# The expert places of an MoE layer: the larger half in order of rank, and the smaller half without the path for many tokens

## The chip, the cores and the metric

One NeuronCore of a Trainium2 chip runs the whole layer. The metric is the device time of one execution in microseconds (us), as the median of several executions of the same program. The profile shows one execution; its times are counted from the first instruction of the program.

## The reference

The layer mixes 512 latent tokens (with 256 context tokens) by retention and mLSTM, and then sends each latent token through two of 32 experts. Only the second half matters here:

```python
g_idx = top_1(softmax(u @ w_rg + b_rg))               # a group of 8 experts for each token
e_idx = top_2(softmax((u @ w_re + b_re)[g_idx]))      # two experts in that group
for each expert e, for the tokens x that chose it:
    y = (silu(x @ w_e1[e]) * (x @ w_e3[e])) @ w_e2[e] # 1024 -> 512 -> 1024, float32
out[token] += weight * y
x = post_norm(DN_ALPHA * x + g2 * out, ln2_g, ln2_b)
```

There are 1024 assignments of a token to an expert, and they are uneven. With the inputs of the reference the experts get between 4 and 144 tokens.

## The kernel before, in words

The kernel does the mixing half first, up to about 1000 us, and then works through 32 **places**, one expert each. The weights of an expert are three pieces of 2 MB (w_e1, w_e3, w_e2), and all 96 pieces must be streamed from HBM. They go through a ring of 11 slots (`RING`): `load(n)` puts piece `n` into slot `n % 11`, on SyncE's (SP's) queue, in order. It waits for two things: that the piece which had the slot is used up, and (line 953) that piece `n - 3` has landed, so that at most three loads are under way. Piece `3e+2+11` is asked for after the last product of place `e`, and pieces `3e+11` and `3e+12` after all first products of place `e`. So the ring holds the place at work and the two and two thirds places behind it.

The tokens of an expert are cut into **blocks** of 32. A place with `n` blocks does for each block: `hidden_q` on TensorE (64 matmul records of `ps_h`, line 1485), the SwiGLU on ScalarE and VectorE (lines 1466 to 1468), two transposes (`turned`, line 1475, with a copy on ScalarE, line 1477), and `product_q` (32 records of `ps_y`, line 1495) whose result VectorE scales into `yt` or `yq` (line 1497). A DMA on GpSimd's (POOL's) queue stores it to `y_d`. The first block's last product is put off into the next place (`finish`), so that TensorE need not wait for the SwiGLU.

The first two blocks of the places from 4 on are fetched by indirect DMAs on POOL (`fetch_both`, line 1444, tile `xr`, three buffers), three places ahead, and transposed on TensorE one place ahead (`facing`, lines 1452 and 1454). Blocks three and up (`xo`) are fetched when the place is at work: `rows` copies a column of the index table to `ix` (line 1507) and gathers by it. Each place runs, in program order: `hidden_q` of block one, `facing` of the next place, `fetch_both` of three places on, `finish` of the place before with its store (line 1646), then a conditional `If(n >= 2)` (line 1668). Inside it stand a nested conditional that fetches four `xo` blocks (lines 1670 to 1673), block two and its store (line 1676), and a nested conditional with `several` (line 1677): block three, and further conditionals for four, five, six and more blocks. All engines run through these conditionals. An engine for which a condition is false takes an other way round the body, on which it waits until everything that the body would have had to wait for or to follow is done. On POOL these are the eight lanes of its DMAs (`DMASW0` to `DMASW7`), each of which carries every eighth DMA. The order of TensorE and SP is the order of the program; POOL's, VectorE's and ScalarE's is chosen by a scheduler. `mark_branch_hint_location` on TensorE announces ahead of a branch where it will go.

Which expert sits at which place is computed on VectorE around 1003 to 1016 us. Places 0 to 3 (`SET`) are experts 0 to 3. The 28 others are ranked by their count (`ov`, 4 for the largest). Ranks 18 to 31, the smaller half, go to the odd places: 31, the smallest, to place 5, and 18 to place 31 (place `67 - 2r`). Ranks 4 to 17, the larger half, go to the even places, nine even places on from one rank to the next: place `4 + 18(r - 4) mod 28`. The `place` table holds for each place the expert, its number of blocks, and the column of its third block.

For the inputs of the reference, counted from its routing, the numbers of blocks at places 0 to 31 are 1111 5111 2121 3111 2121 2131 1121 2121. There are 48 blocks in all. Place 4 has five (144 tokens), places 22 and 12 have three (96 and 71), eight places have two. No place of the smaller half has over 28 tokens.

Of the kernel before, what the change touches and what calls it, by code (L numbers as in the profile page):

```python
# [9 lines left out]
F32 = mybir.dt.float32  # L10
# [9 lines left out]
P = 128  # L20
# [7 lines left out]
RING = (2, 6, 3)  # L28
NC = 112
SET = 4  # L30
YB = 2
ALPHA = 2.0 ** 0.25
EPS = 1e-5
# [35 lines left out]
def build(tc, I, out, dbg=None):  # L69
# [897 lines left out]
    def rows(pool, name, src):  # L967
        t = pool.tile([P, D], F32, name=name)
        SP.dma_start(t, src.rearrange("(o d) -> o d", o=1).to_broadcast([P, D]))
        return t  # L970
# [486 lines left out]
    def stored(o):  # L1457
        for q_ in scat:
            tc.declare_no_dep(o.ins, q_.ins, reason="each slot has its own rows")
        scat.append(o)  # L1460

    def gated(tag):
        return mr.tile([64, 256], F32, tag=tag, name=tag, bufs=1)
# [16 lines left out]
    def hidden_q(x, w, t):  # L1480

        ps = hps.tile([P, 512], F32, tag="ph", name="ps_h")
        for kt in range(NK):
            for a in range(4):
                PE.matmul(ps[32 * a:32 * a + 32, 0:256], x[:, kt % 2, kt // 2, :],  # L1485
                          w[a // 2][:, kt, 256 * (a % 2):256 * (a % 2) + 256],
                          start=(kt == 0), stop=(kt == NK - 1))
        return swiglu(ps, t)
# [10 lines left out]
    def output_q(h, w2, yq):  # L1499
        product_q(turned(h), w2, yq)  # L1500

    def overflow(e):
        return nc.values_load((ocol if e < SET else place[2])[0:1, e:e + 1], min_val=2 * NE, max_val=2 * NE + 32)

# [35 lines left out]
    with tc.manual_schedule(engines={EN.DVE}):  # L1540
# [8 lines left out]
        V.tensor_scalar(ocol, obase, 2.0 * NE, None, op0=OP.add)  # L1549
        V.tensor_scalar(obase, obase, 32.0, 64.0 * NE, op0=OP.mult, op1=OP.add)  # L1550


        key = m1p.tile([P, NE], F32, name="key")
        V.scalar_tensor_tensor(key, cnt, 2048.0, eoff, op0=OP.mult, op1=OP.subtract)
        V.tensor_scalar(key[:, 0:SET], eoff[:, 0:SET], -1.0, 1.0e7, op0=OP.mult, op1=OP.add)
        val = m1p.tile([P, NE], F32, name="val")
        V.tensor_scalar(val, ocol, 1024.0, None, op0=OP.mult)
        V.scalar_tensor_tensor(val, nblk, 32.0, val, op0=OP.mult, op1=OP.add)
        V.scalar_tensor_tensor(val, eoff, 1.0 / 64, val, op0=OP.mult, op1=OP.add)

# [8 lines left out]
            V.tensor_tensor(M, *beside(key[:, h], key, 16), op=OP.is_lt)  # L1569
            V.reduce_sum(ov[:, h], M, axis=AX.X)  # L1570
        place += [m1p.tile([P, NE], I32, name=f"place{a}") for a in range(3)]
        ninths = place[0]
        V.tensor_scalar(ninths, ov, 9.0 * 4682, -9.0 * 4682 * SET, op0=OP.mult, op1=OP.add)
        V.tensor_scalar(ninths, ninths, 16, None, op0=OP.logical_shift_right)
        V.tensor_scalar(nil, ov, SET - 0.5, None, op0=OP.is_gt)
        V.tensor_scalar(eoff, ov, 17.0, SET - 18.0 * SET, op0=OP.mult, op1=OP.add)
        V.scalar_tensor_tensor(eoff, ninths, -28.0, eoff, op0=OP.mult, op1=OP.add)
        V.tensor_mul(nil, nil, eoff)
        V.tensor_scalar(key, ov, (NE + SET) / 2 - 0.5, None, op0=OP.is_gt)
        V.scalar_tensor_tensor(eoff, ov, 3.0, eoff, op0=OP.mult, op1=OP.add)  # L1580
        V.tensor_scalar(eoff, eoff, -1.0, 2.0 * NE + 3, op0=OP.mult, op1=OP.add)
        V.tensor_mul(key, key, eoff)
        V.tensor_add(ov, ov, nil)
        V.tensor_add(ov, ov, key)
# [52 lines left out]

    xr = {e: fetch_both(e) for e in (4, 5)}
    late = []

    def finish():

# [6 lines left out]
    with tc.manual_schedule(engines={EN.PE}):  # L1649
        for e in range(NE):  # L1650
            w = W.pop(e)
            n = nb
            if e + 1 < NE:
                nb = nc.values_load((nblk if e + 1 < SET else place[1])[0:1, e + 1:e + 2], min_val=0, max_val=16)  # L1654
            yt = mr.tile([P, 512], F32, tag="yt", name="yt", bufs=YB)
            yq = mr.tile([P, 256], F32, tag="yq", name="yq", bufs=1)
            xT = xnext
            tc.mark_branch_hint_location(f"more{e}a", smin(n >> 1, 1), engines={EN.PE})
            t0 = hidden_q(xT[0], w, gated("t0"))
            if e + 1 < 4:  # L1660
                xnext = [slots_in(e + 1, b) for b in range(2)]
            elif e + 1 < NE:
                pair = xr.pop(e + 1)
                xnext = [facing(pair[b], b, *((tps, "tp") if e == 3 else (gps, f"g{2 * (e % 2) + b}"))) for b in range(2)]
                if e + 3 < NE:
                    xr[e + 3] = fetch_both(e + 3)
            finish()
            with tc.If(n >= 2, label=f"more{e}a"):  # L1668
                xo = [mr.tile([P, 256], F32, tag=f"xo{a}", name="xo", bufs=1) for a in range(4)]
                with tc.If(n > 2):  # L1670
                    first = overflow(e)
                    for a in range(4):
                        rows(first + a, xo[a])
                tc.mark_branch_hint_location(f"more{e}c", smin(n // 3, 1), engines={EN.PE})
                output_q(hidden_q(xT[1], w, gated("t1")), w[2], yt[:, 256:512])
                stored(G.dma_start(y_d[e * 64 + 32:e * 64 + 64, :].rearrange("s (a f) -> a s f", a=4), yt[:, 256:512]))
                with tc.If(n > 2, label=f"more{e}c"):
                    several(e, w, n, yq, xo)
            late.append((e, turned(t0), w[2], yt))
            for m in range(2):  # L1680
                load(3 * e + m + sum(RING))
        finish()
# [98 lines left out]
```

## Time and profile before

| | |
|---|---|
| time, median of 3 executions | 1633.62 us (1630.96 to 1636.97) |
| the profiled execution: its time, and its span from the first to the last instruction | 1635.97 us, 1634.3 us |
| TensorE busy, weight loads | 1328.7 us (81%), 1024.0 us (63%) |
| VectorE, ScalarE, GpSimd busy | 775.7, 425.2, 300.3 us |
| moved by DMA | 350.38 MB, 214 GB/s in the mean |

The span is the time between the first and the last instruction; the 1.7 us between it and the execution's time lie around it. A rate of some 405 GB/s, at which the 16 DMA engines show as busy all the time, is what the stretches with weight loads reach. The page's slices are 40.9 us each; the 32 places fill the last 16 of them. Names such as `DVE` (VectorE), `ACT` (ScalarE), `PE` (TensorE), `PEq` (TensorE's sequencer) and `POOL` stand as in the profile.

### The profile page before, as it was taken

The page shows a single profiled execution, that of the slowest core. Times are in us where ns is not written, and L with a number is a line of the kernel's source. Part 1 is how long each engine was busy: PE and PEld are TensorE (multiplying, and loading weights), DVE is VectorE, ACT ScalarE, POOL GpSimd, SP SyncE. Part 2 cuts the span into 40 slices and gives each one's busy share as a digit, 9 for nine tenths or more (in the row PEclk, how much of TensorE's full clock was granted, in tenths as well). Part 3 has the DMA queues.
Part 4 walks back from the last instruction along what each step waited for, and adds up shares of the span by engine and source line. Part 5 has one row for each costly group of instructions (what it writes and reads, how often), then busy time and mean ns, then how long its engine had stood idle before and what let it go on. Part 6 is the DMA issues. An engine that isn't in the chain of part 4 may idle for free. (4 is left out here: it accounts for less than half of the span.)

```text
span 1634.3 us, 27557 instructions
## 1 busy us (share of the span) xinstructions
PE 1328.7 (81%) x10733; PEld 1024.0 (63%) x10733; DVE 775.7 (47%) x1863; ACT 425.2 (26%) x764; POOL 300.3 (18%) x260
## 2 busy tenths in 40 slices
PE   5999888999999999999998964557764676637774
PEld 3797877989798998989887753323432343313341
DVE  6657367485656566575777797111110111111115
ACT  3423244353444444444333121000000000000001
POOL 0100046143100000000022243322212212121104
PEclk9999999999999999999999876778776987878797
DMA  9423985253422122121656586864997799959954
GB/s 351 131 64 118 294 252 153 88 174 116 105 72 72 59 91 65 59 72 53 219 168 207 199 320 259 335 238 180 412 408 314 310 410 410 399 208 406 413 215 159
DMA packets 160925, 350.38 MB, mean 214 GB/s; under 512 B 25629, under 2 KB 112905, under 8 KB 152473
## 3 DMA queue, kind: packets, MB, share of 16 engines
q1 hardware_dynamic: 147736, 328.40, 55.1%
q0 software_dynamic: 11632, 14.68, 2.8%
q10 hardware_dynamic: 1296, 4.19, 0.6%
q8 instruction: 120, 1.97, 0.5%
q14 instruction: 141, 1.15, 0.2%
HBM read 316.34 MB, written 35.69 MB: 215 GB/s over the span
## 5 line engine op out<-in xcount | busy, mean ns | idle before, releaser
L1485 PE MATMUL ps_h<-w,xT 128*32 128x256 f32 x3072 | 225.9, 455 | 20.2 <-issue 18.3
L1485 PEld LDWEIGHTS ps_h<-w,xT 128*32 128x32 f32 x3072 | 124.5, 130 | 109.1 <-issue 72.3
L1454 DVE COPY xT<-ps_x 128x256 f32<-128x256 f32 x63 | 26.3, 418 | 275.2 <-PE ps_x L1452 275.2
L196 DVE TENSOR_TENSOR w_lo<-raw,w_hi 128x1024 fp32r<-128x1024 f32 x96 | 126.9, 1346 | 28.5 <-ACT w_hi L195 28.4
L1475 PE MATMUL ps_ht<-small,t 64*128 64x64 f32 x96 | 17.0, 265 | 137.7 <-PEq L1668 43.0
L1495 PE MATMUL ps_y<-w,hT 128*32 128x256 f32 x1536 | 111.1, 433 | 7.9 <-ACT hT L1477 4.1
L1475 PEld LDWEIGHTS ps_ht<-small,t 64*128 64x128 f32 x96 | 10.9, 159 | 162.5 <-issue 160.6
L195 ACT ACTIVATE w_hi<-raw 128x1024 fp32r<-128x1024 f32 x96 | 96.1, 1050 | 57.8 <-PE ps_t L216 18.1
L1466 ACT ACTIVATE t<-ps_h 64x256 f32<-64x256 f32 x48 | 18.1, 377 | 332.3 <-PE ps_h L1485 308.3
L909 POOL TENSOR_TENSOR raw<-raw,g 128x2048 f32<-128x2048 f32 x4 | 18.5, 4620 | 445.5 <-PE ps_b L216 411.6
L1444 POOL DMA_INDIRECT xr<-u_d,inv x56 | 58.0, 1035 | 221.4 <-DMA xr<-u_d,inv 133.2
L559 POOL TENSOR_TENSOR macc<-macc,mw 128x1024 f32<-128x1024 f32 x32 | 80.7, 2520 | 96.6 <-ACT mw L558 88.9
L1495 PEld LDWEIGHTS ps_y<-w,hT 128*32 128x32 f32 x1536 | 50.8, 121 | 49.3 <-issue 16.1
L215 PE MATMUL ps_q<-u_lat,w_hi 128*128 128x512 f32 x192 | 77.8, 405 | 2.4 <-ACT u_lat L321 1.7
L216 PE MATMUL ps_q<-u_lat,w_hi 128*128 128x512 f32 x192 | 77.1, 402 | 0.0
L217 PE MATMUL ps_q<-u_lat,w_lo 128*128 128x512 f32 x192 | 76.8, 400 | 0.0
L1477 ACT ACTIVATE hT<-ps_ht 128x128 f32<-128x128 f32 x48 | 13.3, 277 | 232.9 <-PE ps_ht L1475 218.4
L1497 DVE TENSOR_TENSOR yt<-ps_y,g2q 128x256 f32<-128x256 f32 x43 | 18.3, 425 | 113.1 <-DMA y_d<-yt 67.8
L215 PE MATMUL ps_v<-w_hi,u_lat 128*128 128x256 f32 x256 | 71.2, 278 | 0.0
L217 PE MATMUL ps_g<-w_hi,u_lat 128*128 128x256 f32 x256 | 71.1, 278 | 0.0
L216 PE MATMUL ps_g<-w_lo,u_lat 128*128 128x256 f32 x256 | 71.1, 278 | 0.0
L215 PE MATMUL ps_g<-w_hi,u_lat 128*128 128x256 f32 x256 | 71.1, 278 | 0.0
(436 smaller groups left out, 3563.1 us busy)
## 6 DMA issues: line engine op xcount, KB each, us to landing
w<-in_w_e_dram SPq DMA_DIRECT2D x96, 2048.0 KB
raw<-in_w_in_dram SPq DMA_DIRECT2D x40, 1024.0 KB
mw<-in_w_ada_dram SPq DMA_DIRECT2D x32, 512.0 KB
y_d<-plain SPq DMA_DIRECT2D x28, 512.0 KB
wada<-in_w_ada_dram SPq DMA_DIRECT2D x4, 2048.0 KB
y_d<-yt POOLq DMA_DIRECT2D x43, 128.0 KB
tanh_d<-tg SPq DMA_DIRECT2D x16, 256.0 KB
br_d<-rt SPq DMA_DIRECT2D x16, 256.0 KB
```

Of the source, the lines that this page charges most:

```text
L195: S.activation(h_, r_, AF.Copy)
L196: V.tensor_sub(l_, r_, f32(h_))
L215: PE.matmul(ps, lh, rh, start=first, stop=False)
L216: PE.matmul(ps, lh, rl, start=False, stop=False)
L217: PE.matmul(ps, ll, rh, start=False, stop=last)
L559: G.tensor_add(acc, acc, w)
L909: G.tensor_mul(raw, raw, g1.rearrange("p (o f) -> p o f", o=1).to_broadcast([P, NK, 256]))
L1444: G.indirect_dma_start(out=xr, out_offset=None, in_=u_d, in_offset=bass.IndirectOffsetOnAxis(ap=at, axis=0), bounds_check=4 * T - 1, oob_i ...
L1454: V.tensor_copy(xT.rearrange("p c a s -> p c (a s)"), pt)
L1475: PE.transpose(pt[:, c, :], h[:, c * P:(c + 1) * P], ident[0:64, 0:64])
L1485: PE.matmul(ps[32 * a:32 * a + 32, 0:256], x[:, kt % 2, kt // 2, :], w[a // 2][:, kt, 256 * (a % 2):256 * (a % 2) + 256], start=(kt == 0), ...
L1495: PE.matmul(py[32 * a:32 * a + 32, 0:256], hT[:, kt % 2, 32 * (kt // 2):32 * (kt // 2) + 32], w2[:, kt, 256 * a:256 * a + 256], start=(kt ...
```

## The change

It has three parts.

1. **Order.** A rank of the larger half goes to place `4 + 2(r - 4)`: the largest to 4, the next to 6, and so on to 30. With these inputs the numbers of blocks become 1111 5131 3121 2121 2121 2121 2111 1111. The odd places stay as they were. VectorE has five small operations fewer for it and three more for `val` (next part).
2. **Rows of blocks three and four in advance.** At the end of place `e`, `fetch_far(e + 1)` fetches two `xo` blocks for place `e + 1` if that is one of the larger half (4, 6, ..., 30) or place 31, whether it has so many blocks or not. An expert with at most two blocks gets the column `EMPTY` (104) in the table, at which no rows stand. Inside the place only blocks five and six are fetched, and only if `n > 4`.
3. **The places 5, 7, ..., 29 (`SMALL`).** They keep block two, in two short conditionals: one around its `hidden_q` right after that of block one, one around its `output_q` and store where the long conditional stood. The nested fetch and `several` are left out there, and so is TensorE's branch hint.

```diff
+SMALL = range(5, 30, 2)
+EMPTY = 104
...
-        V.tensor_scalar(val, ocol, 1024.0, None, op0=OP.mult)
+        V.tensor_scalar(val, ocol, -1.0, float(EMPTY), op0=OP.mult, op1=OP.add)
+        V.scalar_tensor_tensor(val, ov, 0.5, val, op0=OP.is_lt, op1=OP.mult)
+        V.tensor_tensor(val, val, ocol, op=OP.add)
+        V.tensor_scalar(val, val, 1024.0, None, op0=OP.mult)
...
-        ninths = place[0]
-        V.tensor_scalar(ninths, ov, 9.0 * 4682, -9.0 * 4682 * SET, op0=OP.mult, op1=OP.add)
...
-        V.tensor_mul(nil, nil, eoff)
+        V.scalar_tensor_tensor(nil, ov, float(-SET), nil, op0=OP.add, op1=OP.mult)
...
+    def fetch_far(e):
+
+        if SET <= e < NE and e not in SMALL:
+            first = nc.values_load(place[2][0:1, e:e + 1], engines={EN.Pool}, min_val=2 * NE, max_val=EMPTY)
+            far[e] = [rows(first + a, mr.tile([P, 256], F32, tag=f"xo{a}", name="xo", bufs=1)) for a in range(2)]
+
+    def second_block(e, w, n, yt, yq, xT):
+        with tc.If(n >= 2, label=f"more{e}a"):
+            xo = far.pop(e, [])
+            xo += [mr.tile([P, 256], F32, tag=f"xo{a}", name="xo", bufs=1) for a in range(len(xo), 4)]
+            with tc.If(n > (2 if e < SET else 4)):
+                first = overflow(e)
+                for a in range(0 if e < SET else 2, 4):
+                    rows(first + a, xo[a])
+            tc.mark_branch_hint_location(f"more{e}c", smin(n // 3, 1), engines={EN.PE})
+            output_q(hidden_q(xT, w, gated("t1")), w[2], yt[:, 256:512])
+            stored(G.dma_start(y_d[e * 64 + 32:e * 64 + 64, :].rearrange("s (a f) -> a s f", a=4), yt[:, 256:512]))
+            with tc.If(n > 2, label=f"more{e}c"):
+                several(e, w, n, yq, xo)
...
-            tc.mark_branch_hint_location(f"more{e}a", smin(n >> 1, 1), engines={EN.PE})
+            if e not in SMALL:
+                tc.mark_branch_hint_location(f"more{e}a", smin(n >> 1, 1), engines={EN.PE})
             t0 = hidden_q(xT[0], w, gated("t0"))
+            if e in SMALL:
+
+                t1 = gated("t1")
+                with tc.If(n >= 2):
+                    hidden_q(xT[1], w, t1)
...
-            with tc.If(n >= 2, label=f"more{e}a"):
...
+            if e in SMALL:
+                with tc.If(n >= 2):
+                    output_q(t1, w[2], yt[:, 256:512])
+                    stored(G.dma_start(y_d[e * 64 + 32:e * 64 + 64, :].rearrange("s (a f) -> a s f", a=4), yt[:, 256:512]))
+            else:
+                second_block(e, w, n, yt, yq, xT[1])
             late.append((e, turned(t0), w[2], yt))
+            fetch_far(e + 1)
```

The order of instructions shows it best on POOL. Before, at the end of place 5's conditional (`L1668` with all eight lanes is the way of a place with one block round it), POOL's rows are these, up to the conditional of place 6:

```order
L1676 DMA y_d<-yt 4x32x256 [waits DMASW6_49,DVE_49]
L1668 UNCONDITIONAL_BRANCH
L1668 ISA [waits Pool_49,Pool_sequencer_49,DMASW4_49,DMASW5_49,DMASW3_49,DMASW6_49,DMASW2_49,DMASW7_49,DMASW1_49,DMASW0_49]
L1668 UNCONDITIONAL_BRANCH
L1444 DMA xr<-u_d,inv 128x256 [waits DMASW7_49,PE_49]
L1444 DMA xr<-u_d,inv 128x256 [waits DMASW2_49,DMASW0_49,PE_49]
L1646 DMA y_d<-yt 4x32x256 [waits DMASW1_49,DVE_49]
L1654 TENSOR_LOAD place_10123
L1668 COMPARE_AND_BRANCH
```

Now place 5's two conditionals (`L1683`, `L1694`) stand on POOL like this, with the gathers for places 8 and 9 and the store of place 4's first block around them:

```order
L1683 COMPARE_AND_BRANCH
L1683 UNCONDITIONAL_BRANCH x2
L1446 DMA xr<-u_d,inv 128x256 [waits DMASW5_49,PE_49]
L1446 DMA xr<-u_d,inv 128x256 [waits DMASW6_49,PE_49]
L1694 COMPARE_AND_BRANCH
L1696 DMA y_d<-yt 4x32x256 [waits DMASW7_49,DVE_49]
L1694 UNCONDITIONAL_BRANCH
L1694 ISA [waits DMASW7_49]
L1694 UNCONDITIONAL_BRANCH
L1665 DMA y_d<-yt 4x32x256 [waits DMASW0_49,DVE_49]
L1446 DMA xr<-u_d,inv 128x256 [waits DMASW1_49,PE_49]
L1446 DMA xr<-u_d,inv 128x256 [waits DMASW2_49,PE_49]
```

The way round the short conditional waits for one lane, that of the store which it leaves out, where the long one waited for all eight. The even places keep the long one.

Before, the gathers of blocks three to six stood inside the place's conditional, two index copies at a time. POOL, place 4:

```order
L1670 COMPARE_AND_BRANCH
L1503 TENSOR_LOAD place_10124
L1507 ISA
L1507 COPY ix<-inv 128x1 [waits DMASW6_49,DMASW2_49,Pool_49]
L1507 ISA
L1507 COPY ix<-inv 128x1
L1444 DMA xo<-u_d,ix 128x256 [waits DMASW6_49,Pool_49]
L1444 DMA xo<-u_d,ix 128x256 [waits DMASW7_49,Pool_49]
L1507 ISA
L1507 COPY ix<-inv 128x1 [waits DMASW6_49]
L1444 DMA xo<-u_d,ix 128x256 [waits DMASW0_49,Pool_49]
```

Now the two gathers for place 6 stand right behind place 4's conditional, ahead of both conditionals of place 5:

```order
L1647 UNCONDITIONAL_BRANCH
L1647 ISA [waits Pool_49,Pool_sequencer_49,DMASW4_49,DMASW5_49,DMASW3_49,DMASW6_49,DMASW2_49,DMASW7_49,DMASW1_49,DMASW0_49]
L1647 UNCONDITIONAL_BRANCH
L1509 ISA
L1509 COPY ix<-inv 128x1 [waits DMASW2_49,DMASW3_49,DMASW0_49,Pool_49]
L1509 ISA
L1509 COPY ix<-inv 128x1 [waits DMASW4_49,DMASW1_49]
L1446 DMA xo<-u_d,ix 128x256 [waits DMASW3_49,PE_49,Pool_49]
L1446 DMA xo<-u_d,ix 128x256 [waits DMASW4_49,PE_49,Pool_49]
L1673 TENSOR_LOAD place_10126
```

They moved from inside a place to more than one place ahead of it, and `PE_49` among their waits is the use of the same two `xo` buffers by the place before. On TensorE the first short conditional of a small place stands between `hidden_q` and `facing`, the second between `finish` and `turned`; each has its own way round, which waits for TensorE's own earlier matmuls.

More of the change, by code (lines that the diff above doesn't have):

```diff
@@ L1571, in build @@
         place += [m1p.tile([P, NE], I32, name=f"place{a}") for a in range(3)]
-        ninths = place[0]
-        V.tensor_scalar(ninths, ov, 9.0 * 4682, -9.0 * 4682 * SET, op0=OP.mult, op1=OP.add)
-        V.tensor_scalar(ninths, ninths, 16, None, op0=OP.logical_shift_right)
         V.tensor_scalar(nil, ov, SET - 0.5, None, op0=OP.is_gt)
-        V.tensor_scalar(eoff, ov, 17.0, SET - 18.0 * SET, op0=OP.mult, op1=OP.add)
-        V.scalar_tensor_tensor(eoff, ninths, -28.0, eoff, op0=OP.mult, op1=OP.add)
-        V.tensor_mul(nil, nil, eoff)
+        V.scalar_tensor_tensor(nil, ov, float(-SET), nil, op0=OP.add, op1=OP.mult)
         V.tensor_scalar(key, ov, (NE + SET) / 2 - 0.5, None, op0=OP.is_gt)
-        V.scalar_tensor_tensor(eoff, ov, 3.0, eoff, op0=OP.mult, op1=OP.add)
-        V.tensor_scalar(eoff, eoff, -1.0, 2.0 * NE + 3, op0=OP.mult, op1=OP.add)
+        V.tensor_scalar(eoff, ov, -4.0, 2.0 * (NE + SET) - 1, op0=OP.mult, op1=OP.add)
         V.tensor_mul(key, key, eoff)
@@ L1639, in build @@
     late = []
+    far = {}
+    def fetch_far(e):
[15 more added lines that the diff above has]
+                several(e, w, n, yq, xo)
     def finish():
@@ L1667, in build @@
             finish()
[L1668 to L1678, printed above, removed]
+            if e in SMALL:
[4 more added lines that the diff above has]
+                second_block(e, w, n, yt, yq, xT[1])
             late.append((e, turned(t0), w[2], yt))
+            fetch_far(e + 1)
             for m in range(2):
```

## The prediction

> **What bounds the kernel now.** I read the page's slices first. From 1000 us on the 32 places fill the last 16 of the 40, and the DMA row there is high but broken:
>
> ```profile
> DMA  9423985253422122121656586864997799959954
> ```
>
> The view of busy time in stretches, cut at those breaks, shows the weight stream (columns: stretch, length, busy time of each engine, TensorE's granted clock, share of the DMA engines, GB/s):
>
> ```profile
> 1087.00:1125.00 38.00, 27.32 (x334) 12.84 (x334) 5.48 (x13) 2.24 (x7) 11.10 (x19) 0.78 0.13 42
> 1127.00:1254.00 127.00, 86.59 (x1108) 46.39 (x1100) 19.17 (x49) 6.92 (x21) 24.31 (x27) 0.78 1.02 410
> 1257.00:1275.00 18.00, 9.10 (x102) 4.29 (x102) 1.85 (x5) 0.65 (x2) 2.81 (x5) 0.67 0.06 21
> 1277.00:1440.00 163.00, 102.73 (x1405) 57.18 (x1394) 24.33 (x62) 8.88 (x27) 34.22 (x40) 0.82 1.01 407
> 1442.00:1460.00 18.00, 8.60 (x102) 4.06 (x102) 2.02 (x5) 0.65 (x2) 2.42 (x4) 0.69 0.04 15
> 1462.00:1574.00 112.00, 80.22 (x1014) 43.52 (x1009) 19.62 (x54) 6.26 (x19) 19.00 (x23) 0.85 1.00 404
> ```
>
> DMA is saturated in three stretches and nearly idle in three. The idle ones are places 4, 12 and 22, those with five and three blocks: the ring is full and no slot comes free until the crowded place is done. So the stage is bound by DMA, and by TensorE's lag where a crowded place comes. With a ring of eight free pieces such a place would cost little if TensorE arrived there with little lag. It doesn't, because something holds it to the pace of DMA. The view of waits, from 1030 to 1600 us, names it (us in total, times, longest):
>
> ```profile
> POOL xr L1444 <- DMA xr<-u_d,inv: 133.2, 10, 15.2
> DVE yt L1497 <- DMA y_d<-yt: 67.8, 7, 15.7
> PE ps_ht L1475 <- PEq L1668: 43.0, 13, 5.0
> PE ps_x L1452 <- DMA xo<-u_d,ix: 41.8, 3, 23.1
> PE ps_ht L1475 <- DVEq L1677: 25.7, 7, 8.3
> PE ps_ht L1475 <- PEq L1527: 2.0, 1, 2.0
> ```
>
> and POOL's own timeline shows the mechanism (start, us, then idle before):
>
> ```profile
> 1348.45 0.72 POOL L1676 DMA_DIRECT2D y_d<-yt  x1 [13.27 <-DVE t L1468]
> 1349.47 1.08 POOL L1444 DMA_INDIRECT xr<-u_d,inv  x1 [0.30 <-issue]
> 1350.86 1.04 POOL L1444 DMA_INDIRECT xr<-u_d,inv  x1 [0.30 <-issue]
> 1351.89 0.77 POOL L1646 DMA_DIRECT2D y_d<-yt  x1
> 1367.80 1.05 POOL L1444 DMA_INDIRECT xr<-u_d,inv  x1 [15.14 <-DMA xr<-u_d,inv]
> ```
>
> POOL issues two gathers and a store, and then stands for 13 to 15 us: the way round the conditional waits for all eight lanes, so for these transfers to land behind the weight loads. That is a loop of 16 to 18 us a place, no faster than DMA. Stores come late by it, VectorE waits for `yt`, and TensorE for VectorE.
>
> **What a place costs TensorE.** From its timeline, starts of `hidden_q` of places 8, 9, 10 and 12, and what ended places 12 and 22:
>
> ```profile
> 1162.04 5.89 PE L1485 MATMUL ps_h<-w,xT 128*32 128x256 f32 x64 [0.37 <-issue]
> 1180.47 5.22 PE L1485 MATMUL ps_h<-w,xT 128*32 128x256 f32 x64 [0.33 <-issue]
> 1190.63 5.26 PE L1485 MATMUL ps_h<-w,xT 128*32 128x256 f32 x64 [0.45 <-issue]
> ...
> 1229.79 6.15 PE L1485 MATMUL ps_h<-w,xT 128*32 128x256 f32 x64 [0.38 <-issue]
> 1263.29 0.66 PE L1452 MATMUL ps_x<-small,xo 128*128 128x128 f32 x2 [16.55 <-DMA xo<-u_d,ix]
> 1276.39 3.66 PE L1485 MATMUL ps_h<-w,xT 128*32 128x256 f32 x64 [0.43 <-issue]
> ...
> 1411.42 3.66 PE L1485 MATMUL ps_h<-w,xT 128*32 128x256 f32 x64 [0.48 <-issue]
> 1448.61 0.66 PE L1452 MATMUL ps_x<-small,xo 128*128 128x128 f32 x2 [23.13 <-DMA xo<-u_d,ix]
> 1461.21 3.66 PE L1485 MATMUL ps_h<-w,xT 128*32 128x256 f32 x64 [0.44 <-issue]
> 1472.99 2.36 PE L1485 MATMUL ps_h<-w,xT 128*32 128x256 f32 x20 [0.38 <-issue]
> ```
>
> Two blocks (place 8) take 18.4 us and one (place 9) 10.2, so an undisturbed pair takes 28.6. Places 8 to 11 took 67.75, or 33.9 a pair, with the waits above in it. Place 12 took 46.60 and place 22 took 49.79; without their waits for `xo`, 30.05 and 26.66, so 28.4 in the mean. Place 4, and SP's weight loads:
>
> ```profile
> 1073.93 5.58 PE L1485 MATMUL ps_h<-w,xT 128*32 128x256 f32 x64 [0.40 <-issue]
> 1093.04 0.41 PE L1452 MATMUL ps_x<-small,xo 128*128 128x128 f32 x2 [2.16 <-DMA xo<-u_d,ix]
> 1126.43 1.94 PE L1485 MATMUL ps_h<-w,xT 128*32 128x256 f32 x16 [0.29 <-issue]
> ```
>
> ```profile
> 1133.88 113.85 SPq L951 DMA_DIRECT2D w<-in_w_e_dram  x22
> 1282.56 137.62 SPq L951 DMA_DIRECT2D w<-in_w_e_dram  x26
> 1467.39 80.61 SPq L951 DMA_DIRECT2D w<-in_w_e_dram  x16
> 1552.79 0.38 SPq L951 DMA_DIRECT2D w<-in_w_e_dram  x1
> ```
>
> Place 4 took 52.5 us with only 2.16 of waiting for rows. The three rows of SP give 332.08 us less three issues of 0.3 for 61 steps: 5.42 us a load in the saturated stretches, with the gathers and stores that share them, 16.3 a place and 32.5 a pair. An undisturbed pair on TensorE is faster than that, one at the present pace slower.
>
> **The change part by part.**
>
> *VectorE's table.* Two operations fewer in all, and one register load on POOL per place of the larger half. Rows of the same kind:
>
> ```profile
> 1007.56 0.17 DVE L1576 TENSOR_SCALAR eoff<-ov 128x32 f32<-128x32 f32 x1
> 1048.68 0.30 POOLq L1654
> ```
>
> That is 0.4 us less on VectorE, and 15 x 0.30 = 4.5 us on POOL, most of it between the scatter and the reading of its index table, where POOL waits for DMA. I take 0 for both; the bounds are -0.4 and +4.5, if all the loads lay on the path to the first gather.
>
> *Gathers in advance.* Thirty gathers in advance and two inside place 4, each with its index copy, instead of twelve. A gather takes POOL 1.05 us and 0.30 ahead of it (its rows above), so with the copies a pair of places gets about 3 us more on POOL. That is hidden as long as POOL's loop is shorter than the 32.5 us of a pair on DMA: one full wait of 13 to 15, the two `xo` gathers 3, four `xr` gathers 5.4 and three stores 2.3 make 24 to 26 us. Without that cover it would cost up to 3 us x 14 = 42 us. What goes are the waits of 2.16, 16.55 and 23.13 us. The gathers for places 6 and 8 are issued behind the conditional of the crowded place before; the small place's 10.2 us and some 18 us of two blocks lie between them and their use, against the 13 to 15 us that transfers take to land. They stand ahead of the `xr` gathers and of the store of the crowded place's first block, which thus come 3 us later on POOL; `xr` is used a place or more on, and the store's buffer two places on.
>
> *Small places.* POOL's full wait goes at 13 places, and with it, by half, the loop that holds TensorE to 33.9 us a pair. On TensorE one hinted jump becomes two without a hint. Price of a jump: the hinted ones are the 13 waits of 43.0 us, 3.3 each and at most 5.0; one unhinted jump, out of the sixth block at place 4, is 2.0. The new ones skip 64 and 34 matmul records, not some hundreds. I take the pair of jumps at what one costs now, so 10.2 us for the place; the bounds are 3.3 less and 2 x 5.0 - 3.3 = 6.7 more.
>
> *The order.* Place 4 ends at 1126.43 - 2.2 = 1124.3, with DMA idle as before. Then places 5 to 9 have 1, 3, 1, 3, 1 blocks: 10.2 + 28.4 + 10.2 + 28.4 + 10.2, so place 10 begins at 1211.7. In each of the two stretches of 38.6 us that end with a crowded place, six pieces come free: 32.5 us of transfer, 6.1 us idle. Together 12 us in place of 18 x 0.94 + 18 x 0.96 = 34 us at places 12 and 22. From the end of place 8 (1201.5) a pair frees six pieces in 28.6 us, less than the 32.5 that they take, so DMA runs through. Piece 35 goes out at 1201.5 and piece 95 sixty loads later, at 1201.5 + 325 = 1527; it was 1552.79.
>
> *The end.* Before, TensorE was behind when the last piece came:
>
> ```profile
> 1584.39 3.66 PE L1485 MATMUL ps_h<-w,xT 128*32 128x256 f32 x64
> ...
> 1593.17 1.93 PE L1495 MATMUL ps_y<-w,hT 128*32 128x256 f32 x32
> ```
>
> The last product ended at 1595.1, 42.3 us after piece 95 was asked for; 39.2 us remain to the end of the span. Now TensorE alone would be there at 1211.7 + 8 x 28.6 + 5 x 10.2 + 10.7 = 1502 (eight pairs to place 26, five single blocks, and the 10.7 from place 31's start to the last product). So it waits for DMA: three loads under way make 16 us from issue to landing, and 2 us for the product: 1545. With the tail of 39.2 the span is 1584, and 1.7 around it make 1586 against the profiled 1635.97. That execution lies 2.4 us over the median, so I say **1583 us**.
>
> **The rivals.**
>
> *The pace stays (chance 0.2).* If the pairs go on at 33.9 us, because the stores and the remaining full wait at each even place hold VectorE as before, TensorE sets the end: places 5, 7 and 9 at 11.8 (place 23, 1461.21 to 1472.99), place 10 at 1216.5, then 8 x 33.9 + 5 x 11.8 + 10.7, so 1557, and 1596 us in the median's terms. For it speaks that 67.8 us of waits for `yt` stand on stores that stay. Against it, POOL's sum of 24 to 26 us. A rule of the Trainium skill points here ("DMA: Bandwidth & Descriptors", "Queues, rings and completion order"): a DMA engine takes turns between its queues after each packet, so a gather on POOL's queue needn't wait for whole loads on SP's, and half the full waits would be little to win. The 13 to 15 us that POOL stands after each gather don't look like that.
>
> *The rows don't come in advance (0.1).* If the scheduler's place for the new gathers lets them wait behind the stores of the place before, the waits of 16.55 and 23.13 come back, now in a row: place 10 at 1251, DMA idle 40 us longer, 1583 + 40 = 1623.
>
> *Slower (0.06).* The jumps of the small places, 13 x 2 without a hint, while DMA is saturated. TensorE's sum of 1502 has 93 us to the present 1595; over 13 places that is 7.2 us each. So from a price of (7.2 + 3.3) / 2 = 5.2 us a jump on, the kernel is slower. At 6.5 us it would be 1502 + 13 x 9.7 = 1628 for the last product, and 1667 us. Against it: the one unhinted jump of 2.0 us, and no jump over 5.0. The Trainium skill ("Runtime: NRT & Kernel Launch", "Instruction fetch mechanics") has a rule on this: a taken branch whose target lies outside a window of two pages of 256 instructions must first fetch its page. By it a missing hint is a danger for long jumps, while most of the short ones would be free, and TensorE's sum would be 1502 - 13 x 3.3 = 1459 with DMA still setting the end; no row here shows a short jump on TensorE.
>
> *No change (0.04):* the sum of a half-kept pace and a part of the waits for rows.
>
> **How the numbers follow.** The forecast itself has 0.6. About 0.5% (8 us) is what a measurement of this kernel can tell from no change. All cases but the last two are faster by more, so faster 0.9, same 0.04, slower 0.06. The range takes in the pace that stays (1596) and part of the late rows; down, the loads at 5.19 us each, as 2.097 MB at 404 GB/s, make 60 x 0.23 = 14 us less, and 6 us less for the landing. So 1563 to 1612.
>
> **What would show it.** Right: no stretch of idle DMA after place 9 (about 1210 us); no wait for `xo` over 3 us; POOL's full wait once in two places; piece 95 asked for near 1527; the last product within 20 us of that. Wrong: pairs on TensorE still at 33 us with a full ring; waits of `ps_ht` or `ps_x` for TensorE's sequencer at lines 1683 and 1694 of 5 us; waits for `xo` of 15 us at places 6 and 8.

## The result, and the profile after

| | before | after |
|---|---|---|
| median, beside each other (4 executions each) | 1632.47 us (1630.96 to 1636.97) | 1596.11 us (1595.53 to 1598.43) |
| the profiled execution: time, span | 1635.97 us, 1634.3 us | 1595.84 us, 1594.2 us |
| TensorE and GpSimd busy | 1328.7 and 300.3 us | 1317.7 and 323.0 us |

The ratio is 0.9775, with an interval of 0.9753 to 0.9798. The forecast was 1583 us, with a range of 1563 to 1612. What follows shows that the total came out near the forecast for reasons that differ from the ones given: one of the three parts brings all of it.

The page's slices after. The holes at the 31st, 32nd and 36th slice are closed (a slice is 39.9 us now):

```profile
DMA  9423985343512222121365656892899999999954
```

The view of busy time in stretches, cut where the stream of weights changes (columns as in the prediction: busy times, clock, share of the DMA engines, GB/s). The first row lies in place 4, the third is the end of place 8 and the start of place 9:

```profile
1087.00:1119.00 32.00, 22.75 (x328) 11.35 (x320) 5.48 (x13) 1.97 (x6) 9.94 (x17) 0.90 0.14 42
1121.00:1188.00 67.00, 54.17 (x774) 29.49 (x774) 13.43 (x34) 4.96 (x15) 19.60 (x27) 0.92 1.00 388
1188.00:1200.00 12.00, 7.94 (x128) 4.88 (x132) 2.13 (x6) 0.93 (x3) 2.03 (x4) 1.00 0.70 255
1200.00:1360.00 160.00, 121.40 (x1680) 66.84 (x1676) 28.86 (x73) 10.48 (x32) 52.48 (x66) 0.87 1.02 407
1360.00:1518.00 158.00, 104.75 (x1228) 50.65 (x1220) 23.18 (x62) 8.15 (x25) 35.35 (x46) 0.75 1.02 406
```

After place 4, DMA is idle for 12 x 0.30 = 3.6 us, where it was idle for 34 us before. The view of waits (from 1060 us; us in total, times, longest):

```profile
POOL y_d L1656 <- DMA y_d<-yt: 77.2, 7, 13.5
DVE yt L1499 <- DMA y_d<-yt: 28.0, 3, 16.5
PE ps_h L1487 <- DMA w<-in_w_e_dram: 27.9, 11, 5.2
PE ps_z L1733 <- DMA x<-x_d: 14.0, 1, 14.0
PE ps_ht L1477 <- PEq L1694: 10.1, 12, 2.6
PE ps_x L1454 <- PEq L1683: 2.0, 12, 0.2
PE ps_x L1454 <- DMA xo<-u_d,ix: 1.5, 1, 1.5
```

POOL stands at the places of the larger half (line 1656) and no longer at each. TensorE has no long wait for `xo`. It waits for weights 11 times, which it never did in this stretch before: the ring runs empty, so DMA sets the pace. The two short jumps of a small place (lines 1683 and 1694) cost 12.1 us over 12 places. POOL's timeline from place 18 to place 20 shows the full wait, two places of issues, and the next full wait:

```profile
1341.61 0.72 POOL L1656 DMA_DIRECT2D y_d<-yt  x1 [12.64 <-DMA y_d<-yt]
...
1355.62 1.05 POOL L1446 DMA_INDIRECT xr<-u_d,inv  x1 [4.16 <-PE ps_x L1454]
...
1358.21 0.77 POOL L1665 DMA_DIRECT2D y_d<-yt  x1 [0.24 <-DVE yt L1499]
1369.70 0.72 POOL L1656 DMA_DIRECT2D y_d<-yt  x1 [10.72 <-DMA y_d<-yt]
```

SP's loads: piece 35, then `x1` of the tail ahead of piece 95, and piece 95:

```profile
1193.25 0.39 SPq L953 DMA_DIRECT2D w<-in_w_e_dram  x1
```

```profile
1514.07 0.39 SPq L1713 DMA_DIRECT2D x<-x_d  x1
1518.43 0.38 SPq L953 DMA_DIRECT2D w<-in_w_e_dram  x1
```

And TensorE's timeline at the end, from the last product of place 29 to that of place 31:

```profile
1519.25 1.93 PE L1497 MATMUL ps_y<-w,hT 128*32 128x256 f32 x32
1535.21 6.45 PE L1733 MATMUL ps_z<-x,small 128*128 128x512 f32 x8 [14.02 <-DMA x<-x_d]
1542.11 0.30 PE L1477 MATMUL ps_ht<-small,t 64*128 64x64 f32 x2 [0.45 <-PEq L1647]
...
1550.88 1.93 PE L1497 MATMUL ps_y<-w,hT 128*32 128x256 f32 x32
```

The span fell by 40.1 us: piece 95 is asked for 34.4 us earlier (1552.79 to 1518.43), the last product ends 34.4 us behind it in place of 42.3, and the tail takes 41.4 us in place of 39.2. But TensorE stood for 14 us ahead of the last work of place 30 and of place 31. That TensorE follows the order of the program holds only for the loop over the places; what stands behind the loop, the scheduler may move into it. It had put four products of the tail's sum (`ps_z`, an identity times `x1`, eight matmul records) ahead of place 30's transposes, and they need a transfer of 2 MB that was issued at 1514.07.

### The profile page after: what moved, and what is told of

It reads as the page before. It is cut to its first block, busy times and chain, and to the rows that moved or that the text cites. A ratio compares the mean times of both kernels' runs of the same rounds, so it can differ in the third digit from the quotient of the medians.

```text
span 1594.2 us, 27616 instructions
## 1 busy us (share of the span) xinstructions
PE 1317.7 (83%) x10733; PEld 1013.2 (64%) x10733; DVE 777.3 (49%) x1861; ACT 425.3 (27%) x764; POOL 323.0 (20%) x300
## 5 line engine op out<-in xcount | busy, mean ns | idle before, releaser
L1487 PEld LDWEIGHTS ps_h<-w,xT 128*32 128x32 f32 x3072 | 119.2, 128 | 136.1 <-issue 62.2
L1469 DVE SCALAR_TENSOR_TENSOR t<-t,ps_h 64x256 f32<-64x256 f32 x48 | 19.6, 409 | 195.1 <-ACT t L1468 195.1
L1497 PE MATMUL ps_y<-w,hT 128*32 128x256 f32 x1536 | 104.0, 413 | 7.0 <-ACT hT L1479 5.1
L1477 PE MATMUL ps_ht<-small,t 64*128 64x64 f32 x96 | 16.4, 256 | 101.2 <-DVEq L1647 31.5
L1477 PEld LDWEIGHTS ps_ht<-small,t 64*128 64x128 f32 x96 | 10.6, 152 | 125.1 <-issue 125.1
L1497 PEld LDWEIGHTS ps_y<-w,hT 128*32 128x32 f32 x1536 | 48.7, 116 | 44.7 <-issue 10.1
```

The source lines that it names most:

```text
L1469: V.scalar_tensor_tensor(t, t, 1.0, ps[0:64, 0:256], op0=OP.add, op1=OP.mult)
L1477: PE.transpose(pt[:, c, :], h[:, c * P:(c + 1) * P], ident[0:64, 0:64])
L1497: PE.matmul(py[32 * a:32 * a + 32, 0:256], hT[:, kt % 2, 32 * (kt // 2):32 * (kt // 2) + 32], w2[:, kt, 256 * a:256 * a + 256], start=(kt ...
```

## The experiments

Each kernel was timed beside the kernel before, on the same chip, and the ratio is to that (its medians lay between 1632.5 and 1637.8 us, so ratios compare better than times). First the three parts in all combinations. The column of idle DMA is worked out from the stretches of busy time at the two crowded places behind place 4, as length times what is missing of the share.

| parts | median us | ratio (interval) | DMA idle at the two places, us |
|---|---|---|---|
| none (before) | 1632.47 | 1 | 34 |
| 1 (order) | 1627.39 | 0.9928 (0.9896 to 0.9961) | 27 |
| 2 (rows in advance) | 1629.94 | 0.9975 (0.9954 to 0.9997) | 31 |
| 1 and 2 | 1627.06 | 0.9941 (0.9912 to 0.9969) | 23 |
| 3 (short conditionals) | 1596.25 | 0.9768 (0.9738 to 0.9799) | 0 |
| 1 and 3 | 1608.03 | 0.9836 (0.9801 to 0.9872) | 12 |
| 2 and 3 | 1594.61 | 0.9738 (0.9705 to 0.9770) | 0 |
| all (after) | 1596.11 | 0.9775 (0.9753 to 0.9798) | 4 |

**Part 1 alone.** The new order in the kernel before:

```diff
-        ninths = place[0]
-        V.tensor_scalar(ninths, ov, 9.0 * 4682, -9.0 * 4682 * SET, op0=OP.mult, op1=OP.add)
...
-        V.tensor_mul(nil, nil, eoff)
+        V.scalar_tensor_tensor(nil, ov, float(-SET), nil, op0=OP.add, op1=OP.mult)
...
+        V.tensor_scalar(eoff, ov, -4.0, 2.0 * (NE + SET) - 1, op0=OP.mult, op1=OP.add)
```

> The kernel before with part 1 alone (the larger half in order of rank). Theory (the order needs the rows in advance and a faster POOL): the waits for xo of 15 to 23 us stand at places 6 and 8 in a row, DMA idles there for about 50 us in place of 34 us at places 12 and 22, pairs stay near 34 us, TensorE behind at the end: 1625 to 1645 us, so no gain. Rival A (the order alone removes the idle time): 1600 us or less.

Its stretches at places 6 and 8:

```profile
1148.00:1170.00 22.00, 8.91 (x102) 4.29 (x102) 1.69 (x4) 0.66 (x2) 5.49 (x9) 0.69 0.38 150
...
1198.00:1219.00 21.00, 11.17 (x134) 4.98 (x125) 2.53 (x6) 0.66 (x2) 6.22 (x10) 0.67 0.35 139
```

22 x 0.62 + 21 x 0.65 = 27 us of idle DMA: the idle stretches have only moved. The time, 1627.39 us, was in the theory's range and a little under that of the kernel before (0.9928). The theory's sizes were not: it had 50 us of idle DMA, and waits for `xo` of 15 to 23 us, which came to 22.9 us in three, the longest 12.4.

**Parts 2 and 3, old order.** The lines of VectorE's table are put back:

```diff
+        ninths = place[0]
...
-        V.scalar_tensor_tensor(nil, ov, float(-SET), nil, op0=OP.add, op1=OP.mult)
+        V.tensor_scalar(eoff, ov, 17.0, SET - 18.0 * SET, op0=OP.mult, op1=OP.add)
+        V.scalar_tensor_tensor(eoff, ninths, -28.0, eoff, op0=OP.mult, op1=OP.add)
+        V.tensor_mul(nil, nil, eoff)
...
```

> The changed kernel with the old order of the larger half (places nine even places on), rows in advance and short conditionals kept. Theory: without the wait for xo a place with three blocks takes 24 to 31 us, and a ring with TensorE close behind it covers that, so places 12 and 22 no longer idle DMA; the order is worth under 6 us: 1588 to 1602 us. Rival A (the order carries the gain): the idle stretches at places 12 and 22 come back, 1612 us or more.

As the theory had it: no idle DMA at places 12 and 22, and no more time than with the new order.

**Parts 1 and 3, rows fetched inside the place.**

```diff
+FAR = ()
...
-        if SET <= e < NE and e not in SMALL:
+        if e in FAR:
...
-            with tc.If(n > (2 if e < SET else 4)):
+            with tc.If(n > (4 if e in FAR else 2)):
...
-                for a in range(0 if e < SET else 2, 4):
+                for a in range(2 if e in FAR else 0, 4):
```

> The changed kernel with blocks three to six fetched inside the place again, as before. Theory: waits for xo of 15 to 23 us at places 6 and 8, place 10 about 35 to 40 us later than 1203.6, DMA idle there, pairs on at 30 us afterwards: 1620 to 1636 us. Rival (fetching in advance is hidden anyway, the order and POOL carry it): 1600 us or less.

The waits for `xo` didn't come back, and the theory falls. The time, 1608.03 us, lies between the theory's and the rival's:

```profile
PE ps_x L1455 <- DMA xo<-u_d,ix: 9.6, 5, 3.6
```

9.6 us in five pieces, though the rows are fetched inside the place as before. So the waits of 16.55 and 23.13 us before were not the price of a late fetch as such. POOL came to that fetch late, out of the full wait of the place ahead. In the kernel before, place 12 began at 1229.79, and POOL's rows there are:

```profile
1251.42 1.05 POOL L1444 DMA_INDIRECT xr<-u_d,inv  x1 [15.17 <-DMA xr<-u_d,inv]
...
1255.02 1.06 POOL L1444 DMA_INDIRECT xo<-u_d,ix  x1 [0.16 <-POOL ix L1507]
```

**Parts 1 and 2, long conditionals at all places.**

```diff
-SMALL = range(5, 30, 2)
+SMALL = ()
...
+FAR = (4, 6, 8, 10, 12, 14, 16, 18, 20, 22, 24, 26, 28, 30, 31)
```

> The changed kernel with the long conditional at the places of the smaller half too (POOL's full wait at each place again), order and rows in advance kept. Theory (POOL's full wait sets the pace): two waits of 13 to 15 us and 11 us of issues make a loop of 37 to 40 us a pair, over the 32.5 us of DMA; places 10 to 25 take 290 us or more in place of 242.5, the ring stays full, 1615 to 1640 us. Rival (the wait is not what paces TensorE): pairs at 30 to 33 us, 1594 to 1602 us.

The time is in the theory's range, its pace isn't: from place 10 to place 26 it took 266.7 us (1220.5 to 1487.2 by its timeline), 33.3 us a pair and not 36. Against the changed kernel, piece 35 goes out 17.7 us later (at 1210.92), after 23 us of idle DMA at places 6 and 8. Piece 95 goes out 26.6 us later (at 1545.00), since the stream itself is slower here: sixty loads take 334.1 us in place of 325.2. POOL stands in front of the very gathers that were to be early:

```profile
POOL ix L1510 <- DMA xr<-u_d,inv: 83.1, 8, 13.1
...
POOL ix L1510 <- DMA y_d<-yt: 63.6, 5, 14.5
```

**Part 3 alone.** The kernel before with the short conditionals (the diff of part 3).

> The kernel before with part 3 alone (short conditionals at the odd places 5 to 29). Theory: the idle stretches at places 12 and 22 stay or grow, since xo is still fetched inside the place; piece 95 is asked for near 1545, TensorE comes through the rest faster than before and ends 20 to 35 us behind it in place of 42: 1605 to 1628 us. Rival (POOL's full wait is the whole matter): 1600 us or less.

The rival held: 1596.25 us, the whole gain. Its stretches at places 12 and 22, and its waits:

```profile
1204.00:1237.00 33.00, 23.70 (x312) 12.48 (x314) 5.30 (x13) 2.24 (x7) 9.34 (x14) 0.84 1.02 411
...
1366.00:1408.00 42.00, 25.65 (x306) 12.88 (x310) 5.29 (x13) 2.24 (x7) 8.32 (x14) 0.76 1.02 413
```

```profile
DVE yt L1500 <- DMA y_d<-yt: 21.8, 2, 16.8
...
PE ps_x L1455 <- DMA xo<-u_d,ix: 9.6, 4, 5.4
```

All stretches from 1118 to 1510 us show a DMA share of 1.01 or more: DMA is not idle behind place 4, with the crowded places where they were and their rows fetched when they are at work. Piece 95 is asked for 8 us earlier than in the changed kernel, and the last product ends 40.4 us behind it:

```profile
1510.04 0.38 SPq L954 DMA_DIRECT2D w<-in_w_e_dram  x1
```

**Part 2 alone.** Rows ahead in the kernel before (`FAR` with places 4, 6, ..., 30 and 31, `SMALL` empty, old order).

> The kernel before with part 2 alone (rows of blocks three and four fetched a place ahead, old order, long conditionals at every place). Theory: the waits of 16.55 and 23.13 us go, but POOL's loop becomes 37 to 40 us a pair and holds TensorE, so little is won: 1612 to 1640 us. Rival B (the whole gain is the two waits for rows, whose 39.7 us come close to the 36 us that were won): 1592 to 1602 us.

The time, 1629.94 us, is in the theory's range, but neither of its steps held. The waits for `xo` didn't go, they were cut up:

```profile
PE ps_x L1455 <- DMA xo<-u_d,ix: 36.3, 6, 12.0
```

And the pairs between the crowded places took 32.3 us (places 14 to 22, 1273.23 to 1402.43), which is no loop of 37 to 40. POOL's rows show why the waits stayed. Place 12 began at 1220.89, and its gathers, written at the end of place 11, were issued only behind that place's full wait:

```profile
1241.59 0.36 POOL L1510 COPY ix<-inv 128x1 int32 x2 [12.60 <-DMA xr<-u_d,inv]
1242.66 1.06 POOL L1447 DMA_INDIRECT xo<-u_d,ix  x1 [0.70 <-POOL ix L1510]
```

A fetch that is written a place ahead still comes late when the engine that issues it stands in a full wait in between.

**Part 3 with POOL's full wait put back.** At each place 5 to 29 a conditional that is never entered stands behind the store of block two. Its body is POOL's alone; the other engines only branch past it:

```diff
                 with tc.If(n >= 2):
                     output_q(t1, w[2], yt[:, 256:512])
...
+                with tc.If(n > 2):
+                    for a in range(8):
+                        fetch(inv[:, a:a + 1], "xr2")
```

> The kernel before with part 3 alone, as in the run of that name, and one thing more: at each place 5 to 29 of the smaller half a conditional that is never entered stands on GpSimd, with eight gathers in it, so that its way round waits for all eight lanes again. TensorE's, VectorE's and ScalarE's short conditionals stay, and so do the places of their work. Theory (POOL's full wait at each place is what part 3 removes): waits of 10 to 15 us behind xr at 13 places come back on POOL, pairs go back to 33 us or more, 1620 to 1640 us. Rival (the gain of part 3 is in the shorter jumps, or in block two's products that come earlier): 1590 to 1604 us.

1640.32 us, ratio 1.0024 (0.9987 to 1.0061): all of the gain is gone, with TensorE's short jumps still there. The early products of block two can't be the gain either: with these inputs no odd place has a second block, so they never run. Its idle stretches are back at places 12 and 22, and so are the waits:

```profile
1244.00:1268.00 24.00, 11.55 (x111) 5.07 (x107) 2.11 (x5) 0.66 (x2) 6.37 (x10) 0.64 0.36 145
...
1428.00:1452.00 24.00, 9.50 (x90) 4.43 (x94) 2.11 (x5) 0.66 (x2) 5.62 (x10) 0.60 0.33 126
```

```profile
DVE yt L1500 <- DMA y_d<-yt: 137.9, 12, 22.3
POOL y_d L1672 <- DMA xr<-u_d,inv: 113.8, 12, 12.4
...
PE ps_x L1455 <- DMA xo<-u_d,ix: 24.6, 3, 13.7
```

This run and the one with part 3 alone differ in little else than POOL's work: the other engines have one branch more at 13 places, on TensorE 0.2 us each. So the gain lies in what POOL does at the small places. They don't differ in the wait alone, though. The scheduler put the store of the place before (line 1672), which follows two gathers, behind the new wait, where in the kernel before it stood ahead of it. Below is such a store here, and then one in the run with part 3 alone:

```profile
1356.42 0.77 POOL L1672 DMA_DIRECT2D y_d<-yt  x1 [12.37 <-DMA xr<-u_d,inv]
```

```profile
1338.20 0.77 POOL L1672 DMA_DIRECT2D y_d<-yt  x1 [1.25 <-DVEq L1701]
```

That may be why VectorE waits longer for `yt` here than in the kernel before (137.9 us for 67.8). How the loss is shared between the wait itself and the store that it holds back was not separated. Parts 1 and 2 with the long conditionals have the store ahead of the wait and lose most of the gain as well (0.9941), there with TensorE's long jumps; this speaks for the wait.

**Two weight loads under way.** In the kernel before:

```diff
-            tc.add_manual_dep(loads[n].ins, loads[n - 3].ins.name,
+            tc.add_manual_dep(loads[n].ins, loads[n - 2].ins.name,
```

> The kernel before with at most two weight loads under way in place of three (piece n waits for piece n - 2); its order, its rows and its conditionals as they were. Theory (a gather or store queues behind the loads under way, so POOL's full wait is as long as these): POOL's waits fall from 13 to 15 us to 8 to 10, its loop to 11 to 13 us a place, under the 16.3 us of DMA, and pairs to about 30 us; if two loads still keep the engines busy, 1590 to 1612 us. Rival (the engines take turns between the queues, so the loads ahead don't matter): waits of 13 to 15 us as before and 1625 us or more.

Ratio 1.0004 (0.9969 to 1.0040): the theory falls. POOL still stands for up to 15.4 us behind `xr`. The DMA issues of this kernel from 1130 to 1510 us (KB each, median us to landing), and below them those of the kernel with the full wait put back, which has three loads under way:

```profile
w<-in_w_e_dram SPq DMA_DIRECT2D x61, 2048.0 KB, 11.4
y_d<-yt POOLq DMA_DIRECT2D x28, 128.0 KB, 11.1
xr<-u_d,inv POOLq DMA_INDIRECT x42, 10.0
```

```profile
w<-in_w_e_dram SPq DMA_DIRECT2D x64, 2048.0 KB, 16.2
y_d<-yt POOLq DMA_DIRECT2D x29, 128.0 KB, 10.6
xr<-u_d,inv POOLq DMA_INDIRECT x44, 9.1
```

A load lands 4.8 us sooner with one fewer ahead of it, a gather or a store does not. So these don't queue behind the loads under way.

**The products of `x1` last.** The changed kernel, with `ps_z` tied to the last product of place 31, which `product_q` now returns:

```diff
-            product_q(hT, w2, yt[:, 0:256])
+            products.append(product_q(hT, w2, yt[:, 0:256]))
...
-            PE.matmul(ps, ident, x1[:, i, 512 * c:512 * c + 512], start=True, stop=False)
+            with tc.issue_after(products[-1].ins):
+                PE.matmul(ps, ident, x1[:, i, 512 * c:512 * c + 512], start=True, stop=False)
```

> The changed kernel with the eight products of the identity with x1 put behind the last expert product on TensorE; nothing else moves. Theory: in the changed kernel TensorE stands from 1521.2 to 1535.2 for x1 and then runs these products ahead of place 30's transposes and place 31; without that, places 30 and 31 are through their first products when piece 95 lands near 1536, and the last product ends near 1539 in place of 1552.8: 1579 to 1586 us. Rival (place 30 waits for POOL's stores or the landing of pieces anyway): within 4 us of 1596.

1592.63 us (1588.26 to 1607.96), ratio 0.9734 (0.9707 to 0.9761), against 0.9775 (0.9753 to 0.9798): less than the theory had, and the intervals overlap. The profiled execution was the longest of the six, with place 4 taking 60.5 us in place of 48.7; in it the last product ends 26.7 us behind piece 95 in place of 34.4. By itself this run doesn't decide.

**The same, and `x1` loaded behind piece 95.**

```diff
-    SP.dma_start(x1, x1_d.rearrange("(i p) d -> p i d", p=P))
+    with tc.issue_after(loads[95].ins):
+        SP.dma_start(x1, x1_d.rearrange("(i p) d -> p i d", p=P))
```

> As the kernel with the products of x1 last, and the load of x1 issued behind piece 95 on SP's queue, where it stood one load ahead. Theory: piece 95 lands one load (5 us) earlier, the last product with it, while x1 still lands before the rows of the tail are gathered: 3 to 6 us less than with the products last alone, so 1574 to 1582 us. Rival (queues share the engines by packets, so the order of the last two loads changes nothing, or x1 then comes late for the tail): within 2 us of that kernel, or slower.

1594.62 us, ratio 0.9768 (0.9738 to 0.9799): the theory's further 3 to 6 us don't show. In its profiled execution place 31's first products wait for piece 94 until 1534.96, TensorE ends the last product 13.0 us later, and no wait for piece 95 stands between. With `x1` ahead of piece 95 the same way took 15.5 us, of which 1.26 were a wait for piece 95. So an earlier piece 95 had little left to give.

**The products of `x1` last, in the old order.** The edit of the run before last, made to the kernel with parts 2 and 3.

> Parts 2 and 3 with the old order, as in the run without the new order, and the eight products of the identity with x1 behind the last expert product on TensorE. Theory: TensorE's 12.5 us of standing for x1, ahead of places 30 and 31, goes; the last product comes 26 to 32 us after piece 95 is asked for in place of 40.7: 8 to 14 us less, so 1578 to 1588 us. Rival (two blocks at places 28 and 30 keep TensorE behind the last piece anyway): within 4 us of 1594.6.

1585.18 us (1577.42 to 1586.14), ratio 0.9666 (0.9612 to 0.9720), against 0.9738 (0.9705 to 0.9770) without it: the theory's size. The intervals just touch, but the times don't: the six here are at most 1586.14 us, the four without the edit at least 1592.15. TensorE's last rows:

```profile
1532.47 1.94 PE L1497 MATMUL ps_y<-w,hT 128*32 128x256 f32 x32
...
1539.05 3.19 PE L1497 MATMUL ps_y<-w,hT 128*32 128x256 f32 x32 [1.85 <-DMA w<-in_w_e_dram]
1542.17 7.13 PE L1741 MATMUL ps_z<-x,small 128*128 128x512 f32 x16
```

Places 30 and 31 now run while piece 95 is on its way, and the last product waits for nothing but that piece. Piece 95 was asked for at 1516.25, 22.8 us before the last product began.

**Put together.** That kernel, with `x1` behind piece 95 and ranks five even places on:

```diff
-        V.tensor_scalar(ninths, ov, 9.0 * 4682, -9.0 * 4682 * SET, op0=OP.mult, op1=OP.add)
+        V.tensor_scalar(ninths, ov, 5.0 * 4682, -5.0 * 4682 * SET, op0=OP.mult, op1=OP.add)
...
-        V.tensor_scalar(eoff, ov, 17.0, SET - 18.0 * SET, op0=OP.mult, op1=OP.add)
+        V.tensor_scalar(eoff, ov, 9.0, SET - 10.0 * SET, op0=OP.mult, op1=OP.add)
```

> As that kernel, with x1 loaded behind piece 95, and with ranks of the larger half five even places on in place of nine: blocks at places 4, 6, ..., 30 are then 5 2 2 2 1 3 2 2 2 1 3 2 2 1, so that places 29 to 31 have one block each. Theory: no idle DMA at places 14 and 24, piece 95 asked for near 1512, its landing 5 us earlier and TensorE close behind it: last product 22 to 28 us after it, 1572 to 1584 us. Rival (the tail is bound by the stores and gathers behind the last product and by x1): 1586 to 1596 us.

1580.85 us (1576.81 to 1587.54), ratio 0.9657 (0.9603 to 0.9711). It beats both kernels. As the theory had it, piece 95 is asked for at 1511.2, and the last product ends 24.4 us later. Against the run ahead of it, its two further edits show no difference.

## Why the prediction was right, and where it wasn't

**What bounds the stage: right, and it was the whole matter.** The prediction named POOL's full wait as what holds TensorE to the pace of DMA, and said that a crowded place would cost little if TensorE came there with little lag. The run with part 3 alone (0.9768) and the one that puts the wait back (1.0024) show that the gain lies there. The chain in between (a late store, VectorE waiting for `yt`, TensorE behind it) was read from the waits: 67.8 us for `yt` before, 137.9 with the wait put back (and a store behind it), 21.8 without it. It was not tried by itself, with a third `yt` buffer for instance, and so stays argued.

**The step "The order" failed.** The sum took the fall from 34 to 12 us of idle DMA from the new order, as if places 12 and 22 would go on to idle DMA in the old one. It had not carried its own first finding over: once TensorE follows closely, a ring of eight free pieces covers a place of three blocks. At 5.42 us a load the eight are an estimated 43 us of work for DMA, and place 22 took 41.4 us in the run with part 3 alone (1366.44 to 1407.87). So with part 3 the old order has no idle DMA behind place 4 at all. The new one puts two crowded places right behind place 4, where the ring is still full and DMA has little left to load. Without the rows in advance that costs 0.9836 against 0.9768. With them the two orders can't be told apart (0.9775 and 0.9738, with intervals that overlap).

**"What goes are the waits of 2.16, 16.55 and 23.13 us": they went, by another hand.** The prediction gave them to the gathers in advance. With part 3 and no gathers in advance, 9.6 us of such waits are left; with gathers in advance and no part 3, 36.3. The rival that the rows don't come in advance was near the mark for that second kernel (the gathers come late, though out of the full wait and not behind stores alone), but not for the change. Part 2 is worth something beside part 1 (0.9836 to 0.9775); alone it is worth 0.9975, and in the old order beside part 3 its 0.9768 to 0.9738 is within the intervals.

**Loads of 5.42 us: right.** From piece 35 (1193.25) to piece 95 (1518.43) sixty loads took 325.2 us, against 325. That it fits to the last digit is luck, as they took 334.1 us in the run with parts 1 and 2. Piece 35 went out 8 us earlier than 1201.5. Place 4 ended 2.7 us earlier than taken (place 5 starts at 1121.57, not at 1124.3), and places 5 to 8 took 72.9 us (to 1194.44) in place of 77.2, with 3.6 us of idle DMA in place of 12.

**Small places: jumps within the bounds, below the value taken.** The two jumps cost 0.17 and 0.84 us a place, about 1 us in place of the 3.3 that was taken, so the slower rival's price of 5.2 us was far off. Of the twelve waits at the second jump nine are 0.31 to 0.33 us, and three are 2.1 to 2.6. The Trainium skill ("Runtime: NRT & Kernel Launch", "Instruction fetch mechanics") says that a taken branch waits for a fetch where its target isn't in the window of pages at hand. The two groups of waits are in keeping with that, but no run shows where the pages end.

**The end: the term that was mis-sized.** The last product was to end 18 us behind piece 95 and ended 34.4 us behind it, 16.4 us more. The prediction read that TensorE would wait for DMA alone there. Of the 16.4 us, 5.7 are the landing of piece 95, taken at 16:

```profile
w<-in_w_e_dram SPq DMA_DIRECT2D x1, 2048.0 KB, 21.7
```

The other 10.7 us are TensorE, which came from `x1`'s products late to places 30 and 31. The trace of before had the tail's products among the last places' rows, where `x1` had landed by then:

```profile
1570.27 3.67 PE L1712 MATMUL ps_z<-x,small 128*128 128x512 f32 x8 [0.55 <-DVE yt L1497]
```

The prediction left out that the place of these products in TensorE's order is fixed ahead of the run, while TensorE's arrival there is not. In the old order, tying them to the last product took 40.7 us down to 26.0. Of the 8 us that are left over the 18, the landing accounts for 6.8: 22.8 us in place of 16, as `x1` was a fourth transfer under way. The changed kernel's piece 94, issued just ahead of `x1`, landed in 15.8 us; with `x1` behind piece 95, in the last run, it was `x1` that took long, 21.9 us.

So the sum reads: 8.6 us less from the stream, 16.4 more from the end and 2.2 more from the tail (41.4 for 39.2) turn a span of 1584 into 1594. The 2.4 us by which the execution before lay over the median had no counterpart after, which makes 1596 of 1583.

**What would show it.** No long idle stretch after place 9, no wait for `xo` over 3 us, and the full wait once in two places were all seen; piece 95 near 1527 came better, at 1518; "the last product within 20 us of that" did not come. **The pace that stays** was refuted: the starts of place 10 and place 26 on TensorE's timeline are 242.5 us apart, 30.3 a pair, with the ring empty at times:

```profile
1203.63 1.50 PE L1487 MATMUL ps_h<-w,xT 128*32 128x256 f32 x11 [0.31 <-issue]
...
1446.16 1.07 PE L1487 MATMUL ps_h<-w,xT 128*32 128x256 f32 x4 [0.49 <-issue]
```

That the time of this rival, 1596 us, is the measured one is chance.

## What to carry to other kernels

A conditional whose way round waits for every DMA lane is paid by the engine that issues the transfers, at each place where the condition is false; look there first when fetches that are written early come late. Before adding up the parts of a change, ask for each whether its term is still there once the largest of the others has gone: here, with these inputs, two of three terms were largely shadows of the third. Products of a later stage that a scheduler mixes into the last places are harmless while TensorE is late, and become the bound once it is early, so a change that takes lag away should be read at its end for what was hidden by the lag.

## What the runs showed of the hardware that was not expected

With two weight loads of 2 MB under way in place of three, a load landed 11.4 us after its issue in place of 16.2, but a gather 10.0 us (9.1 with three) and a store 11.1 us (10.6). The prediction had these transfers land "behind the weight loads", and read 13 to 15 us of standing as a sign against the rule of the Trainium skill ("DMA: Bandwidth & Descriptors", "Queues, rings and completion order") that a DMA engine takes turns between queues after each packet. The runs agree with that rule. What makes a gather of 128 KB take 9 to 10 us beside the loads stays open. The rule did not make the full waits cheap, though: their 10 to 15 us are long enough whatever sets them.

The third load under way bought no time in the kernel before (1.0004). From 1277 to 1440 us the stream ran at 394 GB/s with two and at 407 with three, so that kernel wasn't bound by its rate.

Place 4 took 48.7 us in the profiled execution of the changed kernel, and 60.5 and 58.9 us in those of the two kernels that differ from it in `x1` alone, though POOL's instructions are the same there. POOL stood 12.2 and 12.5 us for gathers ahead of the `xo` rows in place of 4.4, and TensorE then waited 6.2 and 7.3 us for them. Of these two executions one was the longest of its six and the other the second fastest, so place 4 doesn't explain the spread of 20 us between the executions of one kernel. Why it takes longer there is open.
